# Hidden-state blocks carried whole into the down projection of a macaron block on one core

## The chip, the core and the metric

The kernel runs on one core of a Trainium2 chip. A core has TensorE (PE), which multiplies matrices, VectorE (DVE), ScalarE (ACT), GpSimd (POOL), and SyncE (SP), which here issues nearly all DMA transfers. They run their own instruction streams in order and wait for each other by semaphores. The metric is the device time of one execution in microseconds; the time of a kernel is the median of its runs.

## The reference

One layer, a sequence of 256 tokens, width 2048, all in float32: a SwiGLU FFN, a mixer, a second FFN, each between two RMS norms and added to the residual (the FFNs with weight one half).

```python
def _swiglu(x, w_gate, w_up, w_down):
    return (jax.nn.silu(x @ w_gate) * (x @ w_up)) @ w_down
...
f = _swiglu(_rmsnorm(h, ln_ffn1_pre[l]), ffn1_gate[l], ffn1_up[l], ffn1_down[l])
h = h + MACARON_WEIGHT * _rmsnorm(f, ln_ffn1_post[l])
mx = _hybrid_mixer(_rmsnorm(h, ln_mix_pre[l]), w_in[l], ...)
h = h + _rmsnorm(mx, ln_mix_post[l])
f = _swiglu(_rmsnorm(h, ln_ffn2_pre[l]), ffn2_gate[l], ffn2_up[l], ffn2_down[l])
h = h + MACARON_WEIGHT * _rmsnorm(f, ln_ffn2_post[l])
```

The hidden width of an FFN is 5632. The mixer joins a recurrent branch (RWKV7, a scan over tokens) and a pooling branch with gates. The change touches the two FFNs.

## The kernel before

**Products in two parts.** A float32 matrix is split into a high part (a rounding copy to `fp32r`, on ACT) and a low part (the rest, one subtraction on DVE). A product (`mm3`, line 640) is three matmuls: high by high, high by low, low by high. Weights come in tiles of two 128-row chunks by 512 columns (512 KB) into `w32` (5 buffers); ACT makes `wH`, DVE makes `wL` (5 buffers each). So every weight tile costs one DMA, one pass on ACT and one on DVE before PE can use it; `x` parts are `xH`, `xL`.

**Units.** All other large tiles are "units", 36 of them, 4 KB per partition each. While a gate/up block with a number below `LEND` is planned, its `w32`, `wH`, `wL` tiles may take a unit when their own ring is full and more than `KEEP` units are free.

**An FFN** (`ffn`, line 1013) has 11 gate/up blocks of 512 hidden columns, numbered 0 to 10, and then the down projection. Blocks 0 and 1 are plain. In a block, the gate columns are called `f` and the up columns `l`; in `down` (line 1097), two neighbouring output blocks of 512 are, for a first pair of column blocks (c = 0) and a second (c = 2).

**Quads.** Two neighbouring k chunks, both token halves and both column blocks make eight products. `Columns.pair` does them plainly: two tiles, eight products. A quad does them in seven, by Strassen's scheme in Winograd's form: DVE makes sums and differences of four weight quarters (`t13`, `t4` and one in place), which are then split, and the same sums of the activations (`sums`, line 696, once per two quads) are the other factors. In `ffn` the work of a quad is cut in two: `early` (line 889) does four products while the block before is running, and `late` (line 911) the other three, for which it loads the second rows of the quad again. In `down`, `quad` (line 936) does all seven at once. `GATE1` and `GATE2` say how many quads each gate/up block has, of its eight k pairs; `DOWN1` and `DOWN2` give the quads of either column pair, after how many pairs the first comes, and the distance of the next ones.

**Carrying.** At the end of a gate/up block the product of silu and up (`sg`) is transposed in 32 x 32 squares on DVE, written to a DRAM scratch (`cx`) and read back in four DMAs with the squares in their right places (`x32`). `carry` (line 826) splits this at once into a high and a low part, two units per block that stay until `down` (22 units for 11 blocks). The whole block is given up; where `down` needs `sums` of it, it is fetched a second time (`raws`).

**Order.** The program is planned before it is emitted. The planner (`Plan.simulate`, line 304) has a duration for each instruction and each DMA, a due time for each from what uses it, and gives each engine the instruction due first among those that are ready within 40 us ahead of PE; PE's own order is that of the program text. What it finds is the order of every engine's queue, and of SP's DMA issues; on the chip the queues run in that order and wait for semaphores. Every instruction is issued by the same helper, so the profile puts almost all under one line, L515; groups are told apart by the names of their tiles.

Of the kernel before, what the change touches and what calls it, by code (L numbers as in the profile page):

```python
# [24 lines left out]
NKF = DFF // P  # L25
# [13 lines left out]
STAG = 6  # L39
LEAD = 16  # L40
EDGE = 3
ENDS = 3, 0, 1, 2
TRAIL = 16
# [2 lines left out]
TB = 6  # L46
AHEAD = 40000.0
EASE = 2.0
GATE1 = [0, 0, 3, 4, 3, 4, 4, 3, 4, 3, 4]
GATE2 = [0, 0, 3, 4, 3, 4, 4, 3, 4, 3, 4]  # L50
OUT_QUADS = ((3, 2, 1.0), (3, 1, 1.0))
DOWN1 = ((9, 1, 2.2), (10, 1, 1.3))
DOWN2 = ((9, 1, 2.2), (10, 1, 1.3))
SCRATCH = 1024
SPARE = 1
SPARE2 = 4
# [39 lines left out]


SYNC = 55.0
LAND = 1600.0
LANES = 8  # L100
CARRY = 1800.0
SWITCH = 100.0
RUN = 16
COLD = 4800.0
# [1 line left out]
STAY = 400.0  # L106
TABLES = {AF.Exp: (0,), AF.Sigmoid: (2,), AF.Tanh: (0, 2, 18), AF.Silu: (18,)}
LENT = ("w32", "wH", "wL")
KEEP = 6
LEND = 5  # L110
IN_ORDER = ("w32", "wH", "wL")


class Plan:
# [110 lines left out]
    def cost(s, o, name, w, r, k):  # L225
        psum = any(getattr(s.tiles.get(x.tensor.name), "psum", False) for x in w + r)
        size = lambda ap: math.prod(ap.shape[1:]) if len(ap.shape) > 1 else 1
        n = max([size(x) for x in w + r] or [0])
        o.tab, o.nbytes, o.cfg = None, 0, None
        if name == "dma_start":  # L230
            x = w[0]
            o.nbytes = math.prod(x.shape) * 4
            run = min(min(y.shape[-1] for y in w + r) * 4, 2048)
            o.dur = o.nbytes / (387.0 if run >= 2048 else 387.0 * max(run, 64) * 1.25
                                / (run + 512))
            o.pace = {"SP": 500.0, "ACT": 110.0, "POOL": 600.0}[o.eng]
            return
        if o.eng == "PE":
            c = size(w[0])
            slow = name == "matmul" and r[0].dtype == F32  # L240
            o.pace = 2 * (0.7 * c + 32) / 2.4 if slow else (c + 32) / 2.4
            if name == "transpose" and c == 128:
                o.pace = 88.0
            elif slow and c <= 4:
                o.pace = 223.0
            elif slow and c == 256:
                o.pace = 430.0
            o.dur = o.pace + 165
            m, k = w[0].shape[0], r[0].shape[0]
            o.cfg = (0, 0) if k == 128 and m in (32, 128) else (k, m)  # L250
        elif o.eng == "ACT":
            extra = 90.0 * sum(isinstance(k.get(x), bass.AP) for x in ("scale", "bias"))
            extra += 100.0 if "accum_out" in k else 0.0
            o.tab = TABLES.get(k.get("func"))
            fix = 60.0 if psum else 103.0
            o.pace, o.dur = n / 1.2 + fix + extra, n / 1.2 + fix + 97 + extra
            if psum and n <= 128:
                o.pace, o.dur = 300.0, 380.0
        elif o.eng == "DVE":
            f = 1 / 0.96  # L260
            if name in ("tensor_copy", "tensor_scalar") and not psum:
                f /= 2
            more = 45.0 if name == "scalar_tensor_tensor" else 26.0 if name == "transpose" \
                else 40.0 if name == "tensor_tensor_scan" or n < 256 else 0.0
            o.pace, o.dur = n * f + 75 + more, n * f + 158 + more
        else:
            o.pace = o.dur = {"tensor_tensor": 400 + 160.0 * n,
                              "tensor_copy": 450.0}.get(name, n + 110.0)
# [260 lines left out]
class Block:  # L529
# [116 lines left out]
    def gemm_tok(s, w, c0, at, KT, evac, lead=False, trail=False, xs=None, cw=512):  # L646
        pss = [s.bank() for _ in range(2)]
        ws = {}

        def do(k, h):  # L650
            (wH, wL), (xH, xL) = ws[k], at(k)
            return s.mm3(pss[h][:, :cw], xH[:, h * P:h * P + P], xL[:, h * P:h * P + P],
                         wH, wL, k == 0, k == KT - 1)

        def keep(tiles):
            ws.update((k, (wH, wL)) for k, wH, wL in tiles)

        def both(k0, k1):
            step = 1024 // cw
            for k2 in range(k0, k1, step):  # L660
                s.tick(k2 / KT)
                keep(s.load_w(w, k2, min(step, k1 - k2), c0, cw))
                for k in range(k2, min(k2 + step, k1)):
                    do(k, 0)
                    do(k, 1)

        if trail:
            both(0, KT - TRAIL)
            s.by_half(w, c0, KT - TRAIL, KT, do, keep, lambda h: evac(h, pss[h]))
            return  # L670
        k0 = 0
        if xs:
            s.head(w, c0, KT, do, keep, xs)
            k0 = KT
        elif lead:
            s.by_half(w, c0, 0, LEAD, do, keep)
            k0 = LEAD
        both(k0, KT)
        s.tick(1.0)
        for h in range(2):  # L680
            evac(h, pss[h])

    def by_half(s, w, c0, k0, k1, do, keep, done=None, between=None):
        for k in range(k0, k1, 2):
            keep(s.load_w(w, k, 2, c0, 512, k - k0 >= STAG))
        for h in range(2):
            if h and between:
                between()
            for k in range(k0, k1):
                if not k % 2:  # L690
                    s.tick((h * (k1 - k0) + k - k0) / (2 * (k1 - k0)))
                do(k, h)
            if done:
                done(h)

# [129 lines left out]

    def carry(s, T1, T, raws, j=None):
        x, d = s.carry_raw(T1)
        if j is None:
            T.extend(s.new_T(1))
            j = -1  # L830
        raws.append(lambda: s.fetch(d, 1024, 4).rearrange("p (i a b h t) -> p a b h i t",
                                                          i=4, a=2, b=2, h=2))
        H, L = [t.rearrange("p k (h c) -> p (k h) c", h=2)
                .rearrange("p m (i t) -> p i m t", i=4) for t in T[j]]
        s.split(x.rearrange("p (i m t) -> p i m t", i=4, t=32), H, L)

    def sumsq(s, src, acc):
        s.nc.scalar.activation(out=s.rtmp("junk").bitcast(mybir.dt.bfloat16), in_=src,
# [142 lines left out]
class Kernel(Block):  # L981
# [30 lines left out]

    def ffn(s, wg, wu, wd, uT, rs, gpost, resid, emit, reload, quads, downs, xs=None):
        nc = s.nc
        hT, raws = [], []
        at = s.T_at(uT)
        nb = NKF // 4

# [18 lines left out]
        ev = evac(rs, None)  # L1037
        pss = [], []
# [18 lines left out]
        for b in range(1, nb):  # L1057
            J = jobs[b]
            while s.after and b == 3:
                s.after.pop(0)()  # L1060
            with s.set(lend=b < LEND):
                s.block_seq(J, jobs.get(b + 1),
                            evac([1.0, 1.0] if b > 1 else rs, J.banks))
        s.down(wd, s.T_at(hT), NKF, s.post(gpost, 0.5, resid, emit, reload, xs is None), raws,
               downs)

    def spread(s, rs, out):
        for h in range(2):
# [25 lines left out]
                s.sums(x.rearrange("p (a b) (h t) -> p a b h t", a=2, h=2), su)  # L1094
        return nT

    def down(s, wd, at, KT, ev, raws, plan):
        sm = []
        for c, (nq, first, step) in ((0, plan[0]), (2, plan[1])):
            J = Columns(s, wd, c * 512, wd, c * 512 + 512, at, KT, sm,  # L1100
                        [2 * i for i in range(nq)], s.bank, s.psum)
            quads = list(J.quads)

            def col(b):
                for h in range(2):
                    ev(c + (b == "l"), h, J.banks[f"{b}{h}"])
            done = {"f": False, "q": False}

            def end_f():
                J.plus("f")  # L1110
                col("f")
            stop = KT - (min(TRAIL, KT - 2 * nq) if c else 0)
            seq = [(k, "f") for k in J.rest] + [(k, "l") for k in J.rest if k < stop]
            for i, (k, b) in enumerate(seq):
                J.pair(k, b)
                if quads and i + 1 >= first + step * (nq - len(quads)):
                    k = quads.pop(0)
                    if 2 * len(sm) <= k:
                        s.sums(raws[len(sm) // 2](), sm)
                    J.quad(k)  # L1120
                    if not quads:
                        J.merge()
                        if i + 1 < len(J.rest) and c:
                            J.plus("l")
                            done["q"] = True
                        if i + 1 > len(J.rest):
                            end_f()
                if i + 1 == len(J.rest) and not quads:
                    end_f()
# [6 lines left out]
            def keep(tiles):  # L1136
                ws.update((k, (wH, wL)) for k, wH, wL in tiles)
# [10 lines left out]
            def last(h):  # L1148
                if not done["q"] and not h:
                    add("l0")  # L1150
                ev(3, h, J.banks[f"l{h}"])
            s.by_half(wd, c * 512 + 512, stop, KT, lambda k, h: J.mul(
                f"l{h}", J.rows(k, h), ws[k]), keep, last, between)

    def post(s, gpost, fac, resid, emit, reload, last=False):
# [807 lines left out]
def kernel(tc, x, ln_ffn1_pre, ln_ffn1_post, ffn1_gate, ffn1_up, ffn1_down,  # L1963
# [11 lines left out]
    with ExitStack() as ctx:  # L1975
# [80 lines left out]
        def emit1(h, c, ap):  # L2056
# [3 lines left out]
              at_tok(xr), emit1, load_to(xr, lambda h: x[0, h * P:h * P + P]),  # L2060
              GATE1, DOWN1, (load, turn, squares, finish, scaled))
        uT3, rs3, pre3, _ = s.next_pre(lambda: s.col["ln_ffn2_pre"])
# [9 lines left out]
        def emit(h, c, ap, queue=nc.sync):  # L2072
            queue.dma_start(out=out[0, h * P:h * P + P, c * 512:c * 512 + 512], in_=ap)
        s.ffn(ffn2_gate[0], ffn2_up[0], ffn2_down[0], uT3, rs3, ln_ffn2_post[0],
              at_tok(h2), emit, load_to(h2, lambda h: hsp[1, h]), GATE2, DOWN2)
        s.plan.emit()
# [49 lines left out]
```

## Time and profile before

Median of three runs: 2003.93 us (2002.91 to 2005.33).

| | us |
|---|---|
| profiled execution | 2005.2 |
| its span, first to last instruction | 2003.5 |
| FFN 1: gate/up blocks to the start of down | 0 to 476 |
| FFN 1: first column pair of down | 476 to 590 |
| FFN 2: gate/up blocks to the start of down | 1314 to 1775 |
| FFN 2: first column pair of down | 1775 to 1889 |
| PE busy | 1986.9 |
| DVE busy | 1812.1 |
| ACT busy | 1203.5 |

The gate/up block ends (the transpose of `sg` on DVE) lie, in FFN 1, at 52.9, 105.7, 149, 187, 230, 274, 313, 358, 396, 440 and 472 us. A duration of a matmul in the profile runs from its start to a modelled end, and the next one starts before that end; the distance of the starts is what a matmul costs. Rows of the windows view name a stretch, its length, and the busy time of each engine in it with the number of instructions.

### The profile page before, as it was taken

How to read it: one execution, taken by the hardware profiler on the slowest of the kernel's cores; microseconds unless marked ns; L12 is line 12 of the kernel's file. 1: busy time of each engine (PE TensorE's matmuls, PEld its weight loads, DVE VectorE, ACT ScalarE, POOL GpSimd, SP SyncE). 2: the span in 40 equal slices, each digit the busy share in tenths (PEclk: the TensorE clock that was granted, in tenths of full speed). 3: DMA queues.
4: the chain of work that ended last, by engine and by line, in shares of the span. 5: the costliest groups of instructions: out<-in, count | busy, mean ns of one | idle time of the engine just before them, and what ended most of it. 6: DMA issues, size and time to landing. Idle time of an engine off the chain costs nothing.

```text
span 2003.5 us, 28223 instructions
## 1 busy us (share of the span) xinstructions
PE 1986.9 (99%) x9724; PEld 1637.6 (82%) x9724; DVE 1812.1 (90%) x2293; ACT 1203.5 (60%) x1561; POOL 72.6 (4%) x142
## 2 busy tenths in 40 slices
PE   9999999999999999999999999999999999999998
PEld 7888887888888887888888788878888888788886
DVE  7999899988999988998898789998998999889996
ACT  9565565556655657864764465565555655656553
POOL 0000000000000010001300100010000000000000
PEclk9999999999999999999999999999999999999999
DMA  9878688898767778758566497767786887987674
GB/s 327 283 252 263 221 267 274 260 283 246 235 217 256 258 229 272 223 174 253 166 193 190 140 321 249 240 248 245 249 294 202 272 279 255 274 248 235 218 255 146
DMA packets 271839, 486.40 MB, mean 243 GB/s; under 512 B 24144, under 2 KB 58192, under 8 KB 271696
## 3 DMA queue, kind: packets, MB, share of 16 engines
q1 hardware_dynamic: 268032, 474.76, 74.6%
q0 software_dynamic: 3232, 9.44, 1.4%
q8 instruction: 76, 1.25, 0.3%
q14 instruction: 67, 0.55, 0.1%
q10 hardware_dynamic: 432, 0.40, 0.1%
HBM read 456.86 MB, written 26.61 MB: 241 GB/s over the span
## 4 chain that ended last, share of the span: by engine, by line
PE 81%; DVE 9%; DMA 4%; issue 3%; ACT 2%; SPq 0%; ACTq 0%; POOL 0%; DVEq 0%; POOLq 0%
PE l L515 29%; PE f L515 24%; PE mm L515 20%; PE p L515 6%; DVE wL L515 4%; DMA w<-in_ffn_gate_dram 2%; ACT wH L515 1%; DVE t L515 1%; DMA w<-in_w_in_dram 1%; DVE xL L515 1%; DMA w<-in_ffn_up_dram 1%; DVE w L515 1%; PE pY L515 0%; DVE sg L515 0%; DVE T L515 0%
## 5 line engine op out<-in xcount | busy, mean ns | idle before, releaser
L515 ACT CAST wH<-w 128x1024 fp32r<-128x1024 f32 (+1 forms) x712 | 729.3, 1042 | 508.5 <-DVE w L515 116.1
L515 DVE TENSOR_TENSOR wL<-w,wH 128x1024 fp32r<-128x1024 f32 (+1 forms) x712 | 848.1, 1206 | 92.0 <-ACT wH L515 71.7
L515 PE MATMUL l<-wL,xH 128*128 128x512 f32 x840 | 327.9, 390 | 5.2 <-DVE wL L515 5.2
L515 PE MATMUL l<-wH,xH 128*128 128x512 f32 x840 | 327.3, 390 | 2.0 <-ACT wH L515 2.0
L515 PE MATMUL l<-wH,xL 128*128 128x512 f32 x840 | 326.8, 389 | 0.0
L515 PE MATMUL f<-wL,xH 128*128 128x512 f32 x640 | 249.2, 389 | 0.4 <-DVE wL L515 0.4
L515 PE MATMUL f<-wH,xH 128*128 128x512 f32 x640 | 249.1, 389 | 0.0
L515 PE MATMUL f<-wH,xL 128*128 128x512 f32 x640 | 249.0, 389 | 0.0
L515 PE MATMUL mm<-wH,xH 128*128 128x512 f32 (+1 forms) x568 | 220.1, 387 | 0.3 <-ACT xH L515 0.3
L515 PE MATMUL mm<-wH,xL 128*128 128x512 f32 (+1 forms) x568 | 220.2, 388 | 0.0
L515 PE MATMUL mm<-wL,xH 128*128 128x512 f32 (+1 forms) x568 | 220.0, 387 | 0.0
L515 ACT CAST wH<-t 128x1024 fp32r<-128x1024 f32 (+1 forms) x150 | 154.2, 1028 | 96.4 <-DVE t L515 38.1
L515 DVE TENSOR_TENSOR t<-w,w 128x1024 f32<-128x1024 f32 (+1 forms) x180 | 182.7, 1018 | 22.4 <-DMA w<-in_ffn_down_dram 7.8
L515 DVE TENSOR_TENSOR wL<-t,wH 128x1024 fp32r<-128x1024 f32 (+1 forms) x150 | 178.4, 1189 | 19.5 <-ACT wH L515 11.2
L515 PEld LDWEIGHTS l<-wL,xH 128*128 128x128 f32 x840 | 157.7, 188 | 41.2 <-DVE wL L515 8.9
L515 PEld LDWEIGHTS l<-wH,xH 128*128 128x128 f32 x840 | 157.7, 188 | 36.6 <-ACT wH L515 4.0
L515 PEld LDWEIGHTS l<-wH,xL 128*128 128x128 f32 x840 | 157.7, 188 | 32.2
L515 PEld LDWEIGHTS f<-wL,xH 128*128 128x128 f32 x640 | 120.2, 188 | 25.7 <-DVE wL L515 0.8
L515 PEld LDWEIGHTS f<-wH,xH 128*128 128x128 f32 x640 | 120.1, 188 | 25.0
L515 PEld LDWEIGHTS f<-wH,xL 128*128 128x128 f32 x640 | 120.1, 188 | 24.8
L515 PEld LDWEIGHTS mm<-wL,xH 128*128 128x128 f32 x568 | 106.8, 188 | 21.3 <-DVE wL L515 0.3
L515 PEld LDWEIGHTS mm<-wH,xH 128*128 128x128 f32 x568 | 106.9, 188 | 21.2 <-ACT xH L515 0.7
(318 smaller groups left out, 2749.7 us busy)
## 6 DMA issues: line engine op xcount, KB each, us to landing
w<-in_w_in_dram SPq DMA_DIRECT2D x120, 512.0 KB, 4.4
w<-in_ffn_up_dram SPq DMA_DIRECT2D x112, 512.0 KB, 4.7
w<-in_ffn_gate_dram SPq DMA_DIRECT2D x108, 512.0 KB, 5.3
w<-in_ffn_gate_dram SPq DMA_DIRECT2D x200, 256.0 KB, 4.2
w<-in_ffn_down_dram SPq DMA_DIRECT2D x100, 512.0 KB, 5.1
w<-in_ffn_up_dram SPq DMA_DIRECT2D x192, 256.0 KB, 4.5
w<-in_ffn_down_dram SPq DMA_DIRECT2D x152, 256.0 KB, 4.1
x<-cx SPq DMA_DIRECT2D x176, 128.0 KB, 5.3
```

Source lines behind the costliest of these rows:

```text
L515: ins = o.fn(*[real(x) for x in o.a], **{n: real(x) for n, x in o.k.items()})
```

## The change

- `GATE1`, `GATE2`: blocks 4, 7 and 9 have four quads instead of three. `DOWN1`, `DOWN2`: the first pair has ten quads instead of nine, two pairs apart instead of 2.2. That makes four quads more in each FFN.
- `carry` splits a block at once only where its number is below `KEPT` (4). From the fifth block (number 4) on the whole block stays in its unit. The parts are made when `down` first asks for them (`late_T`), and `sums` takes the whole block from its unit instead of fetching it again.
- The quads of `down` begin at k chunk 16 (block 4) instead of 0, so they use the blocks that are whole. `sums` are now kept by number and made for the pair of quads that needs them. The last eight pairs of the second column pair (`tail`), done one token half after the other, are the last eight of those that no quad takes, and `by_half` takes a list of them.
- `LEND` is 11 instead of 5, so tiles of all gate/up blocks may take units; `KEEP` is 3 instead of 6.
- The planner's costs of a DMA: it lands 1800 ns instead of 1600 ns after its transfer, a transfer runs at 335 instead of 387 bytes per ns, and the reading back of a carried block takes 1200 ns more instead of 1800.

```diff
-GATE1 = [0, 0, 3, 4, 3, 4, 4, 3, 4, 3, 4]
-GATE2 = [0, 0, 3, 4, 3, 4, 4, 3, 4, 3, 4]
+GATE1 = [0, 0, 3, 4, 4, 4, 4, 4, 4, 4, 4]
+GATE2 = [0, 0, 3, 4, 4, 4, 4, 4, 4, 4, 4]
 OUT_QUADS = ((3, 2, 1.0), (3, 1, 1.0))
-DOWN1 = ((9, 1, 2.2), (10, 1, 1.3))
-DOWN2 = ((9, 1, 2.2), (10, 1, 1.3))
+DOWN1 = ((10, 1, 2.0), (10, 1, 1.3))
+DOWN2 = ((10, 1, 2.0), (10, 1, 1.3))
...
-LAND = 1600.0
+LAND = 1800.0
+RATE = 335.0
 LANES = 8
-CARRY = 1800.0
+CARRY = 1200.0
...
-KEEP = 6
-LEND = 5
+KEEP = 3
+LEND = 11
+KEPT = 4
...
-            o.dur = o.nbytes / (387.0 if run >= 2048 else 387.0 * max(run, 64) * 1.25
+            o.dur = o.nbytes / (RATE if run >= 2048 else RATE * max(run, 64) * 1.25
                                 / (run + 512))
...
-    def by_half(s, w, c0, k0, k1, do, keep, done=None, between=None):
-        for k in range(k0, k1, 2):
-            keep(s.load_w(w, k, 2, c0, 512, k - k0 >= STAG))
+    def by_half(s, w, c0, ks, do, keep, done=None, between=None):
+        for i, k in enumerate(ks):
+            keep(s.load_w(w, k, 2, c0, 512, 2 * i >= STAG))
...
     def carry(s, T1, T, raws, j=None):
         x, d = s.carry_raw(T1)
+        view = lambda t: t.rearrange("p (i a b h t) -> p a b h i t", i=4, a=2, b=2, h=2)
         if j is None:
-            T.extend(s.new_T(1))
-            j = -1
-        raws.append(lambda: s.fetch(d, 1024, 4).rearrange("p (i a b h t) -> p a b h i t",
-                                                          i=4, a=2, b=2, h=2))
-        H, L = [t.rearrange("p k (h c) -> p (k h) c", h=2)
-                .rearrange("p m (i t) -> p i m t", i=4) for t in T[j]]
-        s.split(x.rearrange("p (i m t) -> p i m t", i=4, t=32), H, L)
+            j = len(T)
+            T.extend(s.new_T(1) if j < KEPT else [None])
+
+        def parts():
+            if T[j] is None:
+                T[j], = s.new_T(1)
+            H, L = [t.rearrange("p k (h c) -> p (k h) c", h=2)
+                    .rearrange("p m (i t) -> p i m t", i=4) for t in T[j]]
+            s.split(x.rearrange("p (i m t) -> p i m t", i=4, t=32), H, L)
+        if T[j] is None:
+            s.later[j] = parts
+            raws.append(lambda: view(x))
+        else:
+            parts()
+            raws.append(lambda: view(s.fetch(d, 1024, 4)))
...
+        at_h = s.T_at(hT)
+
+        def late_T(k):
+            if hT[k // 4] is None:
+                s.later[k // 4]()
+            return at_h(k)
+        s.down(wd, late_T, NKF, s.post(gpost, 0.5, resid, emit, reload, xs is None), raws,
+               downs, 4 * KEPT)
...
-    def down(s, wd, at, KT, ev, raws, plan):
-        sm = []
+    def down(s, wd, at, KT, ev, raws, plan, q0=0):
+        sm = {}
         for c, (nq, first, step) in ((0, plan[0]), (2, plan[1])):
             J = Columns(s, wd, c * 512, wd, c * 512 + 512, at, KT, sm,
-                        [2 * i for i in range(nq)], s.bank, s.psum)
+                        [q0 + 2 * i for i in range(nq)], s.bank, s.psum)
             quads = list(J.quads)
+            tail = J.rest[-min(TRAIL, KT - 2 * nq) // 2:] if c else []
...
-            stop = KT - (min(TRAIL, KT - 2 * nq) if c else 0)
-            seq = [(k, "f") for k in J.rest] + [(k, "l") for k in J.rest if k < stop]
+            seq = [(k, "f") for k in J.rest] + [(k, "l") for k in J.rest if k not in tail]
...
-                    if 2 * len(sm) <= k:
-                        s.sums(raws[len(sm) // 2](), sm)
+                    if k // 2 not in sm:
+                        at(k)
+                        two = []
+                        s.sums(raws[k // 4](), two)
+                        sm.update(zip((k // 4 * 2, k // 4 * 2 + 1), two))
                     J.quad(k)
```

More of the change, by code (lines that the diff above doesn't have):

```diff
@@ L668, in gemm_tok @@
             both(0, KT - TRAIL)
-            s.by_half(w, c0, KT - TRAIL, KT, do, keep, lambda h: evac(h, pss[h]))
+            s.by_half(w, c0, range(KT - TRAIL, KT, 2), do, keep, lambda h: evac(h, pss[h]))
             return
@@ L675, in gemm_tok @@
         elif lead:
-            s.by_half(w, c0, 0, LEAD, do, keep)
+            s.by_half(w, c0, range(0, LEAD, 2), do, keep)
             k0 = LEAD
@@ L688, in by_half @@
                 between()
-            for k in range(k0, k1):
-                if not k % 2:
-                    s.tick((h * (k1 - k0) + k - k0) / (2 * (k1 - k0)))
+            for i, k in enumerate(ks):
+                s.tick((h * len(ks) + i) / (2 * len(ks)))
                 do(k, h)
+                do(k + 1, h)
             if done:
@@ L1014, in ffn @@
         nc = s.nc
-        hT, raws = [], []
+        hT, raws, s.later = [], [], {}
         at = s.T_at(uT)
@@ L1063, in ffn @@
                             evac([1.0, 1.0] if b > 1 else rs, J.banks))
-        s.down(wd, s.T_at(hT), NKF, s.post(gpost, 0.5, resid, emit, reload, xs is None), raws,
-               downs)
+        at_h = s.T_at(hT)
[5 more added lines that the diff above has]
+               downs, 4 * KEPT)
     def spread(s, rs, out):
@@ L1151, in last @@
                 ev(3, h, J.banks[f"l{h}"])
-            s.by_half(wd, c * 512 + 512, stop, KT, lambda k, h: J.mul(
+            s.by_half(wd, c * 512 + 512, tail, lambda k, h: J.mul(
                 f"l{h}", J.rows(k, h), ws[k]), keep, last, between)
```

## The prediction

> **What bounds the kernel now.** I read the page's totals first, then the chain of waits, then who waits for whom, stretch by stretch.
>
> ```profile
> span 2003.5 us, 28223 instructions
> PE 1986.9 (99%) x9724; PEld 1637.6 (82%) x9724; DVE 1812.1 (90%) x2293; ACT 1203.5 (60%) x1561; POOL 72.6 (4%) x142
> ...
> L515 PE MATMUL l<-wH,xH 128*128 128x512 f32 x840 | 327.3, 390 | 2.0 <-ACT wH L515 2.0
> ...
> 476.55 8.16 PE f L515 x36
> ```
>
> The last row is a piece of the chain: 36 matmuls in 8.16 us, 0.2267 us each from start to start, though each is listed as 390 ns, because they overlap. A product here is three such matmuls (0.68 us). The matmuls stand back to back almost everywhere, so a matmul removed is worth 0.2267 us as long as DVE keeps up. The exceptions come in two stretches, the later gate/up blocks of either FFN:
>
> ```profile
> PE l L515 <- DVE wL L515: 2.1, 4, 0.8
> PE l L515 <- ACT wH L515: 0.4, 1, 0.4
> ...
> PE l L515 <- DVE wL L515: 1.7, 3, 0.8
> PE l L515 <- ACT wH L515: 0.7, 2, 0.5
> ```
>
> These are PE's waits from 225 to 475 us (FFN 1) and from 1567 to 1775 us (FFN 2): 4.9 us in ten waits. A wait is counted from the modelled end of the matmul before, so each hides 390 - 227 = 163 ns more: 6.5 us in all. One of them, on DVE (start, duration) and then on ACT:
>
> ```profile
> 327.87 1.22 DVE L515 TENSOR_TENSOR t<-w,w 128x1024 f32<-128x1024 f32 x1 [1.04 <-DMA w<-in_ffn_gate_dram]
> 329.01 1.22 DVE L515 TENSOR_TENSOR xL<-x,xH 128x1024 fp32r<-128x1024 f32 x1
> 330.14 0.68 DVE L515 TENSOR_TENSOR w<-w,t 128x512 f32<-128x512 f32 x1
> 330.86 0.69 DVE L515 TENSOR_TENSOR t<-w,w 128x512 f32<-128x512 f32 x1
> 332.07 1.23 DVE L515 TENSOR_TENSOR wL<-w,wH 128x1024 fp32r<-128x1024 f32 x1 [0.52 <-ACT wH L515]
> ...
> 330.99 1.05 ACT L515 CAST wH<-w 128x1024 fp32r<-128x1024 f32 x1 [3.64 <-DVE w L515]
> ```
>
> DVE waits 1.04 us for a weight transfer, then spends 1.14 us (start to start) on the low part of a carried block (xL), then makes the sum that ACT needs; ACT has stood 3.64 us; PE waits for both. The transfers are late because they are issued late:
>
> ```profile
> SPq L515 <- DVE wL L515: 857.6, 473, 9.5
> ```
>
> SP's queue waits above all for DVE to free a weight buffer.
>
> **The change, part by part.** *Quads.* The lists add up to 3 more per FFN in gate/up and 1 more per FFN in down: 8, not 16. The trace has one 1024-wide difference per quad:
>
> ```profile
> L515 DVE TENSOR_TENSOR t<-w,w 128x1024 f32<-128x1024 f32 x112 | 136.3, 1217 | 20.7 <-DMA w<-in_ffn_down_dram 7.8 <-DMA w<-in_ffn_gate_dram 6.4 <-DMA w<-in_w_in_dram 5.9
> ```
>
> so 112 become 120. A quad does 7 products in place of 8: 8 x 3 x 0.2267 = **-5.4 us**. Both bounds agree if DVE keeps up. Its price on DVE is one quad of the first down pair:
>
> ```profile
> 477.71 1.22 DVE L515 TENSOR_TENSOR t<-w,w 128x1024 f32<-128x1024 f32 x1
> 478.85 1.22 DVE L515 TENSOR_TENSOR wL<-w,wH 128x1024 fp32r<-128x1024 f32 x1
> 479.98 0.68 DVE L515 TENSOR_TENSOR w<-w,t 128x512 f32<-128x512 f32 x1
> 480.58 1.22 DVE L515 TENSOR_TENSOR wL<-t,wH 128x1024 fp32r<-128x1024 f32 x1
> 481.72 0.68 DVE L515 TENSOR_TENSOR t<-w 128x512 f32<-128x512 f32 x1
> 482.32 1.22 DVE L515 TENSOR_TENSOR wL<-w,wH 128x1024 fp32r<-128x1024 f32 x1
> 483.46 0.68 DVE L515 TENSOR_TENSOR h<-t,h 128x512 fp32r<-128x512 f32 x1
> 484.06 1.22 DVE L515 TENSOR_TENSOR wL<-w,wH 128x1024 fp32r<-128x1024 f32 x1
> 487.97 1.23 DVE L515 TENSOR_TENSOR xL<-x,xH 128x1024 fp32r<-128x1024 f32 x1 [2.70 <-ACT xH L515]
> ```
>
> From 477.71 to 484.06 it takes 6.35 us, against two plain tiles at 1.14 us: 4.07 us more. In gate/up 4.6 us of it falls one block early, in the block before its own. What that meets is in the windows (columns: length, then PE, PEld, DVE, ACT, POOL busy, clock, DMA share, GB/s):
>
> ```profile
> 100.00:140.00 40.00, 40.00 (x178) 33.11 (x177) 39.63 (x42) 27.21 (x31) 0.00 (x0) 1.00 0.82 270
> 149.20:187.30 38.10, 38.10 (x170) 31.55 (x169) 36.16 (x39) 19.74 (x22) 0.00 (x0) 1.00 0.85 275
> 273.70:396.40 122.70, 120.98 (x530) 98.95 (x530) 114.94 (x118) 72.36 (x81) 0.00 (x0) 1.00 0.83 269
> 396.40:476.20 79.80, 79.04 (x349) 65.04 (x348) 70.66 (x76) 48.79 (x54) 0.00 (x0) 1.00 0.88 267
> 476.20:589.80 113.60, 113.60 (x503) 94.10 (x502) 106.59 (x121) 66.86 (x78) 0.00 (x0) 1.00 0.76 231
> ```
>
> The first row shows that DVE can work 39.63 of 40 us, 99%, while PE loses nothing. Block 3 (second row) gets the early part of a quad: DVE 36.2 + 4.6 = 40.8 us, and PE's length rises with four more early products to 60 x 0.68 = 40.8. Blocks 6 to 8 (third row): DVE 114.9 + 2 x 4.6 (early) + 1.7 - 2.3 (one late part for two plain tiles) - 3 x 1.14 (carry splits gone) = 120.1 us, PE 180 x 0.68 = 122.4. That is 98% and 100%: covered, with nothing to spare. I take **+0.5 us** per FFN; bounds 0 and 5.5 (if DVE's idle time of 122.7 - 114.9 = 7.8 us there were all needed, 2.3 being left).
>
> *Whole blocks and lending.* From block 4 on the split into xH and xL leaves gate/up, so the 1.14 us seen above leaves the late chain. Each such block holds one unit instead of two, six or seven units by the end, and these may be lent to the weight rings in every block now, down to three free ones: weight transfers are issued earlier. This acts on both parts of the 6.5 us. What counts against it is traffic: a gate quad loads its second rows twice, 1.5 MB against 1 MB, so a block of four quads moves about 11.5 MB (with 1 MB of carried data) in 40.8 us, 283 GB/s.
>
> ```profile
> w<-in_ffn_gate_dram SPq DMA_DIRECT2D x200, 256.0 KB, 4.2
> ...
> x<-cx SPq DMA_DIRECT2D x176, 128.0 KB, 5.3
> ...
> 1449.00:1487.60 38.60, 38.60 (x172) 31.94 (x171) 36.19 (x38) 17.93 (x20) 0.00 (x0) 1.00 0.87 301
> ```
>
> The last row, a block of FFN 2 with lending, ran at 301 GB/s without a wait of PE. On SP's queue the new quads add 28 issues net, and the second fetch of carried blocks (5 x 4 per FFN, part of the x176) goes: 40 fewer. I take **-5.5 us** of the 6.5; bounds -6.5 and 0.
>
> *The first column pair of down.* All seven late splits fall due here: six more than before (block 10's was here already). DVE: 106.6 + 4.07 (tenth quad) + 6 x 1.14 = 117.5 us. PE: 166 products, 112.9 us. DVE is overbooked by 4.6 us. The sums stay five per FFN. Ahead of it, blocks 9 and 10 have room: DVE 70.7 - 0.6 - 2 x 1.14 = 67.8 us, PE 79.8 - 5 x 0.68 - 0.8 = 75.6. Together 185.3 of 188.5 us, 98%. The splits' input has lain in SBUF for up to 200 us, so the planner may bring them forward, within 40 us; the weight tiles it cannot, there are five buffers. And block 10's split, for which DVE stood idle 2.70 us (row at 487.97), is now asked for only by its pair, eleventh in the order. If half of the 7.8 us ahead is used, 0.7 us is uncovered, and 1% of idle time adds 1.1: **+2 us** per FFN. Bounds: 0; and with nothing brought forward 4.6 + 7.0 - 2.7 (the idle time that row 476.20 has, less the one wait) = 8.9. What is late next is the matmul waiting for the third tile of a quad, and with it all products behind it on PE. The second pair keeps its 10 quads, its step and its tail of eight pairs.
>
> *The planner's constants* (landing, rate, carry) and the lower reserve of free units reorder every queue, in the mixer too. The place there that could move is one at 757 to 764 us:
>
> ```profile
> PE l L515 <- DVE wL L515: 1.4, 2, 1.0
> PE l L515 <- ACT wH L515: 0.9, 1, 0.9
> ...
> 762.00:764.00 2.00, 2.00 (x6) 1.54 (x6) 2.00 (x3) 2.00 (x4) 0.00 (x0) 0.50 0.78 228
> ```
>
> PE waits 2.3 us, and the matmuls after it run at half clock (0.50) for some 3.5 us: about 4 us that another order may save, or cause once more. **0**, bounds -4 and +4.
>
> Sum, against the profiled execution's span: -5.4 - 5.5 + 1 + 4 + 0 = -5.9, so 1997.6. That execution took 2005.2 us, 1.7 around its span and 1.3 over the median of the runs, so I apply the difference to the median: 2003.9 - 5.9 = **1998.0 us**.
>
> **The rivals.** *All is covered.* Both terms of DVE are nothing and all 6.5 us go: 2003.9 - 11.9 = 1992.0. For it: DVE's 99%. Against: it would have to hold that for 300 us.
>
> *The waits stay.* The transfers, not the buffers, are late: DMA share is 0.83 to 0.88 in these blocks, and traffic rises. Then -5.4 + 4 for down: 2002.5. For it: the 1.04 us in the row at 327.87 is a wait for DMA. Against: 301 GB/s without a wait.
>
> *DVE becomes the bound (slower).* In the first pair of down nothing is brought forward, because units (sums, late parts and lent tiles all draw on the same 36) are full just then: 8.9 us in either FFN, all else as in the first rival: 2003.9 - 11.9 + 17.8 = 2009.8. It decides from 5.9 us per FFN (half of 11.9). For it: 117.5 us of work in 112.9. Against: two of the five sums of this pair were made ahead of it already. The Trainium skill (Perfetto Trace Analysis, Identifying the Most-Contended Engine) says the same in general: judge TensorE by LDWEIGHTS busy time, not by matmul time, and relieve the engine with the highest occupancy. By that, 82% stands against DVE's 90%, and quads load the wrong engine; the trace bears it out only in part, since no matmul here follows another sooner than 0.2267 us.
>
> *The order elsewhere turns against it*: the +4 of the last term, 2002.
>
> **How the numbers follow.** Forecast 0.40, all covered 0.20, waits stay 0.22, DVE bound 0.13, order elsewhere 0.05. A difference under 0.2% (4 us) can't be told from none: faster is below 1999.9, slower above 2007.9. The forecast's own spread is some 4 us either way, so 0.32 of its 0.40 is faster; with 0.20 and a little of the waits' case, 0.55. Slower is the DVE case with a little of the last: 0.14; the same, 0.31. The range leaves out a tenth on each side: 1990 (covered, with part of the mixer's 4 us) to 2007 (most of the DVE case); the forecast's own is 1994 to 2002.
>
> **What would show it.** 120 differences, 24 matmuls fewer; no split into xL after block 3 until down, and seven there; PE's waits before the down stages of both FFNs below 1 us each (right) or still over 2 (the waits stay); the first pair of down 113 to 116 us long (right) or over 119 (DVE bound), with PE waiting for wL within it; DVE at 97% or more from block 6 to its end. The forecast is wrong if PE waits in the first pair outgrow the 5.9 us, or if the mixer's length changes by more than 4.

## The result and the profile after

The changed kernel takes 1989.66 us (median of 6 runs, 1988.36 to 1990.44) against 2003.2 us (6 runs, 2002.36 to 2005.33): a ratio of 0.993, with a 95% interval of 0.9918 to 0.9943. That is 13.5 us less where 5.9 were forecast, 0.3 us below the range, and near the rival in which all is covered (1992.0). Its profiled execution took 1989.87 us, with a span of 1988.0.

The page after, totals:

```profile
span 1988.0 us, 28260 instructions
## 1 busy us (share of the span) xinstructions
PE 1976.1 (99%) x9700; PEld 1631.9 (82%) x9700; DVE 1837.8 (92%) x2327; ACT 1220.2 (61%) x1571; POOL 84.4 (4%) x142
...
L517 PE MATMUL l<-wH,xH 128*128 128x512 f32 x828 | 322.2, 389 | 0.0
```

There are 24 matmuls fewer, and DVE is busy for 25.7 us more. It has 34 passes more, net: 22 of 1024 columns at 1.14 us and 12 of 512 at 0.60 from start to start make 32.3 us, near eight quads at 4.07 (32.6). Why the busy time rose by less was not followed up. The view of PE's waits from 225 to 475 us, and from 1560 to 1770 us, has no row any more; nor has that of 470 to 690 us, where the down projection of FFN 1 lies. In the windows view (columns as before), blocks 6 to 8, blocks 9 and 10, the first pair of down in FFN 1 and the one in FFN 2:

```profile
271.90:394.50 122.60, 122.60 (x543) 101.55 (x542) 118.32 (x124) 73.12 (x81) 0.00 (x0) 1.00 0.82 275
394.50:462.90 68.40, 68.40 (x304) 56.65 (x303) 63.63 (x69) 41.38 (x47) 0.00 (x0) 1.00 0.74 242
462.90:575.80 112.90, 112.90 (x500) 93.52 (x499) 109.52 (x123) 72.06 (x80) 0.00 (x0) 1.00 0.68 219
...
1753.60:1866.60 113.00, 113.00 (x501) 93.58 (x500) 109.61 (x124) 71.76 (x80) 0.00 (x0) 1.00 0.68 218
```

PE is busy through every one of them, and DVE for 93 to 97%.

For the comparison of all the kernels each trace is divided at three points that can be found in every one: the start of the first pair of down in FFN 1 (the weight load of its first quad, less twelve matmuls, 2.72 us), the first `rb` transpose of FFN 2, and the start of the first pair of down in FFN 2. That transpose has nearly the same place in PE's order everywhere, but stands eight matmuls earlier in e9, e10 and e5 and ten later in e12; there the point is moved by that (1.7 and 2.3 us). In us:

| kernel | FFN 1 gate/up | first down and mixer | FFN 2 gate/up | second down | span |
|---|---|---|---|---|---|
| before | 468.7 | 850.0 | 449.6 | 235.2 | 2003.5 |
| changed | 462.9 | 847.4 | 443.5 | 234.3 | 1988.0 |
| changed, once more (e0) | 461.8 | 847.1 | 443.5 | 234.3 | 1986.7 |
| quads alone (e1) | 471.0 | 847.6 | 452.4 | 234.4 | 2005.4 |
| lending alone (e9) | 465.3 | 847.4 | 445.8 | 235.2 | 1993.7 |
| lending and quads (e10) | 462.2 | 849.2 | 444.1 | 234.3 | 1989.9 |
| changed, old lending (e3) | 468.6 | 846.2 | 448.9 | 234.3 | 1997.9 |
| changed, only w32 lent (e12) | 462.8 | 849.8 | 443.5 | 234.3 | 1990.4 |
| changed, split at once (e4) | 463.7 | 848.5 | 444.1 | 234.3 | 1990.6 |
| changed, old quads (e2) | 464.1 | 851.4 | 445.5 | 235.2 | 1996.2 |
| changed, old constants (e5) | 462.3 | 846.1 | 443.7 | 234.3 | 1986.4 |
| nothing brought forward (e7) | 464.2 | 853.9 | 443.5 | 237.4 | 1999.1 |
| ten more passes on DVE (e8) | 463.2 | 854.9 | 443.5 | 244.1 | 2005.7 |
| four more quads (e14) | 463.3 | 856.0 | 442.8 | 238.5 | 2000.6 |

Of the change's 15.5 us of span, 11.9 lie in the two gate/up stretches, 2.6 between them, 0.9 in the second down projection. Each row is one execution, and executions of one kernel differ: by 2 us for the changed kernel, by up to 8 for the kernel before, and in e2 they fall into two sets, six from 1994.9 to 1995.7 us and five, the profiled one among them, from 1997.9 to 1999.0.

### The profile page after: what moved, and what is told of

It reads as the page before. It is cut to its first block, busy times and chain, and to the rows that moved or that the text cites. A ratio compares the mean times of both kernels' runs of the same rounds, so it can differ in the third digit from the quotient of the medians.

```text
span 1988.0 us, 28260 instructions
## 1 busy us (share of the span) xinstructions
PE 1976.1 (99%) x9700; PEld 1631.9 (82%) x9700; DVE 1837.8 (92%) x2327; ACT 1220.2 (61%) x1571; POOL 84.4 (4%) x142
## 4 chain that ended last, share of the span: by engine, by line
PE 94%; DVE 2%; ACT 1%; DMA 1%; issue 1%; SPq 0%; POOLq 0%; ACTq 0%; DVEq 0%
PE l L517 34%; PE f L517 30%; PE mm L517 21%; PE p L517 6%; DVE wL L517 1%; DMA w<-in_ffn_gate_dram 1%; DMA w<-in_w_in_dram 1%; PE pY L517 0%; ACT wH L517 0%; PE pA L517 0%; PE tr L517 0%; PE pU L517 0%; DVE AR L517 0%; PE pSa L517 0%; DVE BK L517 0%
## 5 line engine op out<-in xcount | busy, mean ns | idle before, releaser
L517 PE MATMUL l<-wL,xH 128*128 128x512 f32 x828 | 322.2, 389 | 1.0 <-DVE wL L517 1.0
L517 PE MATMUL f<-wL,xH 128*128 128x512 f32 x608 | 236.6, 389 | 0.0
L517 PE MATMUL f<-wH,xH 128*128 128x512 f32 x608 | 236.6, 389 | 0.0
L517 PE MATMUL f<-wH,xL 128*128 128x512 f32 x608 | 236.5, 389 | 0.0
L517 ACT CAST wH<-t 128x1024 fp32r<-128x1024 f32 (+1 forms) x158 | 165.3, 1046 | 84.2 <-DVE t L517 27.8
L517 DVE TENSOR_TENSOR wL<-t,wH 128x1024 fp32r<-128x1024 f32 (+1 forms) x158 | 191.4, 1211 | 9.2 <-PE f L517 4.0
L517 DVE TENSOR_TENSOR t<-w,w 128x1024 f32<-128x1024 f32 (+1 forms) x194 | 195.6, 1016 | 3.6 <-DMA w<-in_ffn_down_dram 1.8
L517 PEld LDWEIGHTS f<-wL,xH 128*128 128x128 f32 x608 | 114.2, 188 | 23.6
L517 PEld LDWEIGHTS f<-wH,xH 128*128 128x128 f32 x608 | 114.1, 188 | 23.7
L517 PEld LDWEIGHTS f<-wH,xL 128*128 128x128 f32 x608 | 114.1, 188 | 23.6
```

The lines of the kernel that those rows point to most:

```text
L517: ins = o.fn(*[real(x) for x in o.a], **{n: real(x) for n, x in o.k.items()})
```

## The experiments

The kernels of one group ran on one chip beside the kernel before; ratios are to that, with 95% intervals, and a difference in us is a ratio times the time of before there. The groups are e1, e3, e4 and e9; e0, e2, e5 and e10; and e7, e8, e12 and e14. The changed kernel, run once more (e0), had 0.9938 (0.9926 to 0.9951), so a difference to it is given by both its ratios where they matter.

### Quads alone

```diff
-GATE1 = [0, 0, 3, 4, 3, 4, 4, 3, 4, 3, 4]
-DOWN1 = ((9, 1, 2.2), (10, 1, 1.3))
+GATE1 = [0, 0, 3, 4, 4, 4, 4, 4, 4, 4, 4]
+DOWN1 = ((10, 1, 2.0), (10, 1, 1.3))
```

(in the kernel before; the same for GATE2 and DOWN2)

> The kernel before with the new quad lists alone (eight quads more; blocks still split at once, old lending, old planner constants). If a quad pays wherever PE is nearly always busy: 24 matmuls less, 2003.2 - 5.4 = 1997.8 us, and PE's waits in the late gate/up blocks stay at about 2.5 us per FFN. If the quads need the room that the changed kernel makes (DVE would have 40 us of work and more in blocks of 40.8 us, splits included): the waits grow and take it back, 2001 to 2006 us.

2010.03 us, ratio 1.0034 (1.0021 to 1.0047): slower, though it has the same 24 matmuls less. (The profiled execution took 2007.15 us, so the trace shows less of the loss than the median does.) PE's waits from 225 to 460 us, and in FFN 2 from 1560 to 1750 us:

```profile
PE l L515 <- DVE wL L515: 4.8, 5, 1.2
...
PE l L515 <- DVE wL L515: 4.2, 4, 1.2
PE l L515 <- ACT wH L515: 1.0, 1, 1.0
```

The waits doubled. Both gate/up stretches grew, by 2.3 and 2.8 us, in spite of nine matmuls less in each. So here the quads were not worth their matmuls by themselves.

### Old lending

```diff
-KEEP = 3
-LEND = 11
+KEEP = 6
+LEND = 5
```

(in the changed kernel)

> The changed kernel with lending as before (blocks 0 to 4 only, six units kept free). If it was the earlier issue of weight transfers from lent units that removed PE's waits in the late gate/up blocks: they come back, some 6 to 7 us, 1996 us. If it was the split of carried blocks leaving those blocks: 1989.7 to 1991 us, with no waits there. Half and half: 1993 us.

2001.01 us, ratio 0.9982 (0.9973 to 0.999): 9 to 10 us of the gain are gone, more than the whole expectation of 6 to 7. The waits are back:

```profile
PE l L517 <- DVE wL L517: 3.3, 5, 0.8
...
PE l L517 <- DVE wL L517: 3.0, 4, 0.8
```

The chain before one of them, in block 6 (start, duration):

```profile
321.52 0.70 DVE t L517
322.23 0.02 issue
322.24 4.16 DMA w<-in_ffn_gate_dram
326.40 0.04 DVEq L517
326.44 0.87 issue
327.30 1.22 DVE t L517
328.52 0.07 DVE wL L517
328.59 0.98 issue
329.57 0.69 DVE w L517
...
330.70 1.06 ACT wH L517
331.76 0.02 issue
331.78 1.24 DVE wL L517
333.02 0.04 issue
333.06 0.73 PE l L517 x2
```

It is the chain of the kernel before (the prediction's rows from 327.87), without the split of a carried block (xL) in it. DVE ends its work on a raw tile, only then the next transfer of gate weights is issued (4.16 us), DVE makes the difference and the sum of the next quad, ACT splits it, DVE takes the low part, PE waits. So these waits need no split; they come with a late transfer. But the split is not without effect here: with it still in gate/up, with the old constants and with the quads of down from block 0, the same quads on the same chip took 2010.03 us (e1), 9.0 more, and the gate/up stretches were 2.4 and 3.5 us longer. Which of these three made that difference was not separated.

That lending lets transfers be issued earlier can be read from the issues themselves. Take the transfers of gate and up weights by their number, and count how many matmuls PE has started at each issue. Between 230 and 460 us they are issued on average 10 us of matmuls (at 0.2267) earlier with lending alone (e9) than in the kernel before, and 12 us earlier in the changed kernel than here. What lending does to ACT is seen in its waits for a quad's sum in blocks 6 to 8, first in the kernel before, then in the changed one, then in this one:

```profile
ACT wH L515 <- DVE w L515: 34.0, 9, 4.7
```

```profile
ACT wH L517 <- DVE w L517: 6.9, 3, 2.4
```

```profile
ACT wH L517 <- DVE w L517: 20.8, 6, 3.9
```

### Split at once

```diff
-KEPT = 4
+KEPT = 11
...
-               downs, 4 * KEPT)
+               downs, 16)
```

> The changed kernel, but every carried block is split at once and fetched a second time for the sums, as before; quads, lending, planner constants and the quads' place in down stay new. If whole blocks matter (1.14 us less on DVE in blocks that are 98% full, and the units that can be lent): the waits come back and grow, 1995 to 2000 us. If not: 1990 to 1991 us.

1991.83 us, ratio 0.9938 (0.9925 to 0.9952), which can't be told from the changed kernel's. PE has no waits in the late gate/up blocks. Once tiles are lent, the whole blocks, which gave the change its name, have no gain that can be shown; from the intervals they are worth less than about 5 us either way.

### Lending alone

```diff
-KEEP = 6
-LEND = 5
+KEEP = 3
+LEND = 11
```

(in the kernel before)

> The kernel before with the new lending alone (all blocks, three units kept free). If lending needs the units that whole blocks set free: little changes, 2001 to 2003 us. If the switch alone is enough: the waits of 6.5 us go, 1996.5 us.

1998.03 us, ratio 0.9968 (0.9955 to 0.998): 6.4 us less, and PE's waits from 225 to 475 us, and from 1550 to 1760, are all gone. The units that whole blocks set free are not needed for that.

### Old quads

```diff
-GATE1 = [0, 0, 3, 4, 4, 4, 4, 4, 4, 4, 4]
-DOWN1 = ((10, 1, 2.0), (10, 1, 1.3))
+GATE1 = [0, 0, 3, 4, 3, 4, 4, 3, 4, 3, 4]
+DOWN1 = ((9, 1, 2.2), (10, 1, 1.3))
```

(in the changed kernel; the same for FFN 2)

> The changed kernel with the old quad lists (eight quads fewer). If the quads pay in full once tiles are lent: 5.4 us slower than the changed kernel, 8.6 us less than before. If they were paid back by stalls: the same as the changed kernel, 14 us less than before. If DVE at 97 to 99% slowed the changed kernel: even faster.

1995.66 us, ratio 0.9975 (0.9966 to 0.9983), beside 1988.89 for the changed kernel in the same group (e0): 6.8 us slower, the quads' 5.4 and 1.4 more. Against e0's row the gate/up stretches are 2.3 and 2.0 us longer, the nine matmuls of either (2.04 us), and the second down projection 0.9. The stretch between is 4.3 us longer, of which 0.7 is the tenth quad; most of the rest lies at 752 to 760 us, where PE waits and then runs at half clock for 3.4 us. Not every execution need have that (the two sets under the table). With lending the quads pay in full.

### Lending and quads, nothing else

> The kernel before with the new lending and the new quad lists, nothing else (blocks split at once and fetched twice, quads of down from block 0, old planner constants). Lending alone gave 0.9968 (6.4 us less), quads alone 1.0034 (6.8 us more). If lending is what lets quads pay: 6.4 + 5.4 = 11.8 us less. If the whole blocks are needed for that, as DVE has 40 us of work and more in blocks of 40.8 us with the split in them: 4 to 8 us less, with PE's waits back in the late gate/up blocks.

(The edits of e1 and e9 together.) 1991.03 us, ratio 0.9949 (0.9937 to 0.9962), 2.1 us over the changed kernel beside it, with intervals that overlap. PE has no wait for a weight from 225 to 690 us. Two sets of constants make four fifths of the gain, and their effects don't simply add: lending turns the quads from 6.8 us lost (e1) into about 4 won (e10 against e9, 3.8 us by ratios, whose intervals overlap, and by spans).

### Old planner constants

```diff
-LAND = 1800.0
-RATE = 335.0
-CARRY = 1200.0
+LAND = 1600.0
+RATE = 387.0
+CARRY = 1800.0
```

> The changed kernel with the planner's old landing, rate and carry costs. If the constants gave the 2 to 3 us by which the result went past quads and waits (a wait of PE at 751 us is shorter there): 2 to 4 us slower than the changed kernel, and the old wait is back. If not: the same within 1 us.

1988.98 us, ratio 0.994 (0.9926 to 0.9953), against 1988.89: no difference. In the table, the stretch with the mixer is 1.0 us shorter than in the changed kernel in the same group (e0), and FFN 2's gate/up is as long.

### Only raw tiles lent

```diff
-LENT = ("w32", "wH", "wL")
+LENT = ("w32",)
```

> The changed kernel, but only raw weight tiles (w32) may take units; the rings of the split parts (wH, wL) stay at five. If lending works because transfers are issued earlier: as the changed kernel, 1989 to 1990 us. If it works because split parts may stand ready deeper (five tiles are less than two quads): PE's waits come back, 1996 to 2000 us.

1990.34 us, ratio 0.9925 (0.9909 to 0.9942): as good as the changed kernel. The late gate/up blocks have no waits, and their transfers are issued 17 us of matmuls earlier than with the old lending (e3), counted as above. So it is the raw tile, and with it the earlier issue of its transfer, that counts; the split tiles need no more than their five buffers.

### Nothing brought forward

```diff
+                if q0 and not c and not i:
+                    s.first = next(o for o in s.plan.ops[n0:] if o.eng == "PE")
...
-                        s.sums(raws[k // 4](), two)
+                        with s.set(behind=s.first if q0 else None):
+                            s.sums(raws[k // 4](), two)
...
-                s.later[k // 4]()
+                with s.set(behind=s.first):
+                    s.later[k // 4]()
```

> The changed kernel, but the late splits and the sums of down may not run before the first matmul of down has. In the changed kernel two splits and two sums per FFN ran earlier, 2 x 1.14 + 2 x 2.7 = 7.7 us of DVE. If bringing work forward is what covers the first pair of down (DVE 109.5 us of 112.9 there): the pair gets 117 us of work and stretches by 4 us or more in either FFN, 8 to 12 us slower than the changed kernel, with waits of PE for wL in the pair. If DVE uses the time before for weight tiles instead and comes out even: within 2 us of the changed kernel.

1998.89 us, ratio 0.9968 (0.9957 to 0.9979): 6 to 8 us over the changed kernel by the ratios, 11 by the spans. PE's waits in the first down projection, 455 to 600 us:

```profile
PE f L517 <- DVE sL L517: 1.6, 1, 1.6
PE f L517 <- ACT sH L517: 1.0, 1, 1.0
PE p L517 <- DVE xL L517: 0.5, 1, 0.5
```

They are waits for the sums and splits that had to stay. The second down projection is 3.1 us longer, the stretch with the first one 6.5; there PE loses 3.9 us in the waits, from start to start, and 1.6 more as it runs at half clock from 472.9 us on, for 3.4 us. So bringing this work forward is what covers the first pair.

### Ten more passes of DVE

```diff
-        V.tensor_tensor(out=t13, in0=va, in1=vb[:, :1].to_broadcast([P, 2, 512]),
-                        op=ALU.subtract)
+        for _ in range(2 if q.more else 1):
+            V.tensor_tensor(out=t13, in0=va, in1=vb[:, :1].to_broadcast([P, 2, 512]),
+                            op=ALU.subtract)
...
+                    s.more = q0 and not c
                     J.quad(k)
```

> The changed kernel with the 1024-wide difference of each quad in the first pair of down done twice: ten more passes of 1.14 us on DVE per FFN, 11.4 us, no other work. This measures how much room DVE has there. If it has the 3.4 us that the pair's window shows (112.9 - 109.5): 8 us per FFN, 16 us slower than the changed kernel. If the planner can also fill the 4.8 us free in blocks 9 and 10: 3 to 4 us per FFN, 7 us slower. If DVE is not near its bound: no change.

2007.43 us, ratio 1.0005 (0.9995 to 1.0015): 13 to 15 us over the changed kernel by the ratios, 17.7 by the spans. The second down projection grew by 9.8 us for 11.4 us of work, the stretch with the first one by 7.5. PE waits, 1750 to 1880 us; after one more wait its clock is halved (last row, a part of the 3.4 us from 1890.2):

```profile
PE l L517 <- DVE h L517: 2.9, 4, 1.0
PE p L517 <- DVE wL L517: 0.6, 2, 0.3
PE l L517 <- ACT h L517: 0.2, 1, 0.2
...
1890.40:1893.40 3.00, 3.00 (x9) 2.32 (x8) 2.96 (x4) 1.99 (x2) 0.00 (x0) 0.50 0.27 85
```

This is the first of the three cases expected. Of the 9.8 us, 7.8 are waits, counted from start to start over the pitch of 0.2267, and 1.6 the half clock; in the first down projection the waits make 6.7 us, without a half clock. So DVE took 3.6 and 4.7 of the 11.4 us without a loss of PE. That is near the 3.4 us that the pair's window had free (112.9 - 109.5): the room left once the planner has done its best.

### Four more quads

```diff
-GATE1 = [0, 0, 3, 4, 4, 4, 4, 4, 4, 4, 4]
-DOWN1 = ((10, 1, 2.0), (10, 1, 1.3))
+GATE1 = [0, 0, 4, 4, 4, 4, 4, 4, 4, 4, 4]
+DOWN1 = ((10, 1, 2.0), (11, 1, 1.2))
```

> The changed kernel with four more quads: block 2 has four in either FFN, the second pair of down has eleven, 1.2 pairs apart. 12 matmuls fewer, 2.7 us. If PE is still the only bound: 2.7 us less than the changed kernel. If DVE, at 97 to 99% in blocks 1 to 8 and 91 to 93% in the second pair, is the bound now: no gain or 1 to 5 us slower, with waits in blocks 1 to 3.

2002.6 us, ratio 0.9987 (0.9978 to 0.9997): 10 to 11 us over the changed kernel, with 12 matmuls fewer. The gate/up stretches stayed (+0.4, -0.7); the second down projection grew by 4.2 us and the stretch with the first by 8.6. PE's waits from 20 to 700 us are now in down:

```profile
PE p L517 <- DVE wL L517: 1.5, 2, 1.0
PE l L517 <- DVE h L517: 0.8, 1, 0.8
PE p L517 <- ACT wH L517: 0.4, 1, 0.4
```

With eleven quads in the second pair PE waits for DVE in down. But that is not all of the 8.6 us: from start to start, PE loses 3.9 in down, 2.3 at 704 to 708 us, and at 757 to 764 us, where the clock is halved again, 2.9 more than in the changed kernel. No faster version followed from here.

## Why the prediction was wrong

**What bounds the kernel**: right. PE stands back to back outside the waits named, and the gain is matmuls left out, waits gone, and a small part in the mixer.

**Quads, -5.4**: right in size (e2: 6.8, with 24 matmuls), and the condition that went with it, "as long as DVE keeps up", was the whole matter: without lending and whole blocks the same quads cost 6.8 us (e1). I had not worked out what they would do by themselves.

**Waits, -5.5 of 6.5**: right in direction, too small. No wait was left. The 6.5 us themselves were too few: the matmul after the one that waited mostly starts 0.11 us late too, and from start to start, over 0.2267, PE lost 3.9 us (225 to 469) and 3.8 us (1560 to 1768) before, 7.7 in all, and nothing after. With 18 of the 24 matmuls, 4.1 us, that makes 11.8 of the 11.9 us in the two gate/up stretches. Two parts were named as the cause. The earlier transfers remove all of these waits by themselves (e9), and raw tiles are enough (e12). The split leaving the chain adds nothing to that (e4, e10); without lending it may have a share in the 9.0 us between e1 and e3. So the two work on the same waits.

**DVE in blocks 3 to 8, +1**: the loads were about right (118.3 us measured in blocks 6 to 8, 96.5% of their length, against 120.1 worked out, 98%), the stall was not there. This 1 us should have been 0: a row of the profile had shown 99% of DVE without a loss of PE.

**The first pair of down, +4**: this is the step that failed most. It said that half of the room ahead is used, 0.7 us stay uncovered, and 1% of idle time adds 1.1. Measured: 112.9 and 113.0 us, no wait. The work worked out, 117.5 us, was even too small: the 6.35 us of a quad end where its last pass starts, so a quad costs 1.14 more, 5.2 over two plain tiles, and the sum is 118.6. Of it, the window of the pair shows 109.5. The low parts of the late splits (xL) and the sums (sL) in the changed kernel:

```profile
429.91 1.22 DVE L517 TENSOR_TENSOR xL<-x,xH 128x1024 fp32r<-128x1024 f32 x1
435.03 1.22 DVE L517 TENSOR_TENSOR sL<-sf,sH 128x1024 fp32r<-128x1024 f32 x1
455.61 1.22 DVE L517 TENSOR_TENSOR xL<-x,xH 128x1024 fp32r<-128x1024 f32 x1
458.48 1.22 DVE L517 TENSOR_TENSOR sL<-sf,sH 128x1024 fp32r<-128x1024 f32 x1
468.60 1.22 DVE L517 TENSOR_TENSOR xL<-x,xH 128x1024 fp32r<-128x1024 f32 x1
```

The pair begins at 462.9: two splits and two sums stand before it. One of its ten 1024-wide differences does too (nine are in its window), one half-width sum, and two of the low parts of weight tiles (44 in the window, where 45 before and one more for the tenth quad make 46). One of the sums is one more than before. Against the reckoning that is 2 x 1.14 + 1.14 + 0.6 + 2 x 1.14, and 2.6 for one sum more, 8.9 us brought forward, more than twice the half (3.9) that I had let it use. The window ahead (blocks 9 and 10) still has 4.8 us free on DVE, so there was more room than I had reckoned too; why was not followed up. The load itself was real, as e7 and e8 show: hold this work back and PE waits for it; add 11.4 us and 6.7 to 7.8 of them appear as waits. The DVE rival's premise, that nothing comes forward, was wrong, and its price of 8.9 us per FFN was too high: e7 lost 3.1 us in the second down projection and 5.5 in the first (waits and half clock), though it held back the splits and sums alone. The pair's start had been read one plain pair and one quad too late, at 476.2 instead of 468.7; the window from there has the same work in it (106.5 us), so this changed nothing in the sum.

**The planner's constants, 0**: by themselves 0 (e5). But the mixer and the first down projection got 2.6 us shorter, 0.7 of it one product. The trace shows where most of the rest lies: at the place named in the prediction, 757 to 764 us. There, from start to start, PE lost 2.4 us in two waits and 1.6 at half clock. After, one wait is left there, and the clock is whole:

```profile
PE l L517 <- DVE wL L517: 1.0, 1, 1.0
...
745.00:766.00 21.00, 20.01 (x88) 16.17 (x87) 20.03 (x26) 17.09 (x28) 0.53 (x1) 1.00 0.75 230
```

That wait costs 1.3 us from start to start, so this place gave 2.7 us; other waits in the mixer, at 1010 us above all, took part of that back. Neither trace of the changed kernel (after and e0) has a half-clock stretch inside PE's work. Whether that belongs to the new order or to the one execution of the kernel before that was profiled stays open: e2 and e14 have such a stretch at nearly the same place. The bounds of 4 us either way held it.

With the terms as measured, -5.4 - 7.7 + 0 + 0 - 1.9 make 15.0 of the spans' 15.5 us. The medians are 13.5 apart, as the profiled execution of the kernel before was 2.0 us over its median of six. Of the 9.1 us between -5.9 and -15.0 the first pair is 4, the waits 2.2, the mixer 1.9 and DVE in blocks 3 to 8 is 1. The range ended too early because its lower end took the case in which all is covered, with only 6.5 us for the waits, and only part of the mixer's spread.

**The other rivals.** That the waits stay since transfers are late for want of bandwidth is refuted: DMA share is 0.82 in blocks 6 to 8 after against 0.83 before, and the waits go with nothing but lending (e9), for which raw tiles are enough (e12). The rule of the Trainium skill that was cited with the DVE rival (Perfetto Trace Analysis, Identifying the Most-Contended Engine) is to relieve the engine with the highest occupancy. By it the quads were the wrong way; with lending they paid (e2), and with four more they no longer did (e14). Here the rule held at the edge that this kernel had almost reached, not by the ranking of 92% against 82%.

## What to carry to other kernels

When a wait ends with a transfer, look at what its issue waited for: here it was a buffer, and a few more raw tiles (not more split ones) removed all waits in the late gate/up blocks and let an engine at 93 to 97% keep pace. An edit that loads the second-busiest engine is to be priced together with the edit that lets this engine work ahead; apart, the two here gave +6.8 and -6.4 us, together about -10. Where work has its input long before, do not take it that a planner leaves the room ahead of a full stretch unused, and measure what room is left by adding passes of known length. And when these are added, count the waits they cause and a halved clock apart: here the first were 7.8 us, the second 1.6.

## What was not expected of the hardware

DVE kept 97% over a stretch of 113 us (109.52 of 112.90) with PE never waiting, and of 11.4 us of work added there 6.7 and 7.8 us came out as waits of PE. ACT had spent 34.0 us of blocks 6 to 8 behind quads whose sums were late; with tiles lent this fell to 6.9 us with 72 to 73 us of work in both.

Short waits of PE can be followed by a half clock. Six of the traces have one stretch inside PE's work with a granted clock of 0.50 (at 760.9 us before, 756.5 in e2, 760.2 in e14, 472.9 in e7, 1214.2 in e12, 1890.2 in e8). Each lasts 3.4 us, and before each PE had lost 2.2 to 3.9 us within 5 us, from start to start. No threshold follows from that: e7 lost 3.1 us at 1765 to 1769 us and kept its clock.
